# Starting the first projection from x with features on the partitions, and applying its norm factor to the products

## The chip, the cores and the metric

One core of a Trainium2 chip runs the whole program: matrix products on TensorE (PE), elementwise work on VectorE (DVE), ScalarE (ACT) and GpSimd (POOL), loads and stores issued by SyncE (SP). The metric is device time in microseconds, the median of three runs.

## What is computed

Two layers of a first block (an even one with forgetting and dilated attention, an odd one with retention), and a second block with a state-space mixer, windowed attention and a gated feed-forward part. S = 256 positions, D = 1024 features, all fp32. The change touches the start of the even layer:

```python
def rms_norm(x, g):
    y = xf * lax.rsqrt(jnp.mean(xf * xf, axis=-1, keepdims=True) + EPS)
    return (y * g).astype(x.dtype)

z = rms_norm(x, g_norm) @ w_in
qa, ka, va, ga, fa, qb, kb, vb, gb = jnp.split(z, cuts, axis=-1)
log_f = jax.nn.log_sigmoid(fa + b_f)
ya = forgetting_attention(hA(qa), hA(ka), hA(va), log_f)
```

The norm factor is one number per position, so it may be applied to a product x·g @ w after the product, row by row.

## The kernel before

Each fp32 operand is split into a high part (fp32r) and the low part that is left, and a product is made of three: high by high, high by low, low by high. For weights the class `Weights` does this tile by tile: `load` issues a 512 KB tile of [128, 1024] on SP, `_prepare` casts it on ScalarE (wh, L73) and takes the low part on VectorE (wl, L78) or, where `plan` is given a share, every second one on GpSimd. `next` keeps two tiles prepared ahead of the one in use. There are five raw buffers and six of wh and wl each, so a load waits for the low part of the tile five before it, and a cast for TensorE's last use of the tile six before it.

x is loaded by rows (positions on the partitions). `norm_transposed` squares and sums the rows (L199, L202), raises to -0.5 on GpSimd (L191), multiplies by factor and gain (L215), turns each 128x128 block on TensorE (L235) and splits the result into xTh and xTl (L242, L243). `first_xs` (L297, L304) makes the first value projection va from them, four weight tiles; `forget_gates` makes 24 small products with w_fa (L251 to L253), a chain of small steps on VectorE and ScalarE (L638 to L645), a copy of the running sums to c_f on GpSimd (L647) and a store to DRAM (L648). `fox_masks` loads these sums back, spread over the partitions (L653), and adds the causal mask on GpSimd (L656, L657); VectorE takes it up in `masked_min` (L354, L356).

Then for each group of heads `proj_ws` makes q, k and the gate g, two halves of eight pairs of products each (L263 with the high weights, L264 with the low ones), evicted by ScalarE and VectorE (L267 to L271) out of three banks, so that a half can start when the half three before it has left its bank. Scores (L346), softmax and the product with v follow one group behind.

Beside all this runs `tables_common`: angles, sines and powers for the state-space mixer far later (L394 to L405, L438 to L540), on VectorE, ScalarE and GpSimd, from the table ssm_par. Its four copies of m on GpSimd (L538) share one buffer, so each waits until SP has stored the one before (L540).

Nothing fixes the order of these on an engine except a few added order rules: a scheduler places every engine's instructions in one list, and an engine runs its list in order. SP's loads and stores are one such list too, and at most eight of them are under way.

Of the kernel before, what the change touches and what calls it, by code (L numbers as in the profile page):

```python
# [19 lines left out]
P = 128  # L20
# [16 lines left out]
KE = ("pp", "py")  # L37
XH = 2
# [7 lines left out]
class Weights:  # L46


    def __init__(self, tc, raw, par, ahead):
        self.tc, self.nc, self.raw, self.par, self.ahead = tc, tc.nc, raw, par, ahead  # L50
        self.after, self.loaded, self.loads, self.lows = [], [], 0, []
        self.jobs, self.shares, self.done, self.used = [], [], [], 0

# [5 lines left out]
    def load(self):  # L59
        ap = self.jobs[self.loads]  # L60
        self.loads += 1
        r = self.raw.tile([P, 1024], F32, tag="raw", name="wraw")
        self.nc.sync.dma_start(r[:, :ap.shape[1]], ap)
        self.loaded.append(r)

    def _prepare(self):
# [6 lines left out]
        i = nc.scalar.copy(h[:, :n], r[:, :n])  # L73
# [5 lines left out]
        self.done.append((h, lo))  # L79

# [19 lines left out]
def model_kernel(ctx: ExitStack, tc: tile.TileContext, a: dict, out: bass.AP):  # L100
# [23 lines left out]
    g_row = nrm.tile([P, D], F32, tag="gain", name="g_row")  # L124
    nc.sync.dma_start(g_row[:1, :], a["even_norm"])
    x = [res.tile([P, D], F32, name=f"x{t}") for t in range(2)]

    def load_x(t):
        for h in range(XH):
            sl = slice(h * D // XH, (h + 1) * D // XH)  # L130
            nc.sync.dma_start(x[t][:, sl], a["x"][t * P:(t + 1) * P, sl])

    load_x(0)
# [36 lines left out]

    w.load()
    load_x(1)


# [30 lines left out]
    def norm_transposed(t, g, th, tl, name, kinds=("pt", "pt"), eng=None, after=None):  # L205

        with tc.high_priority():
            xt = x[t]
            parts = [mean_square(xt[:, h * 512:(h + 1) * 512], D, name, eng if h else None) for h in range(2)]
            r = rstd_from(parts, EPS, name)  # L210
            xn = []
            for h in range(2):
                sl = slice(h * 512, (h + 1) * 512)
                xn.append(nrm.tile([P, 512], F32, tag="xn", bufs=3, name="xn"))
                V.scalar_tensor_tensor(xn[h], xt[:, sl], r, g[h], op0=ALU.mult, op1=ALU.mult)  # L215
            return transposed(xn, 8, th, tl, 0, t, kinds, after)

# [11 lines left out]
    def transposed(src, n, th, tl, k0, t, kinds=("pt", "pt"), after=None):  # L229

        m = min(4, n)
        for b, sb, kind in zip(range(0, n, 4), src, kinds):
            pt = bank(kind)
            for j in range(m):
                i = T.transpose(pt[:, j * P:(j + 1) * P], sb[:, j * P:(j + 1) * P], ident)  # L235
                if after is not None:
                    tc.add_manual_dep(i.ins, after.ins.name, NOSYNC, reason="order")
                    after = None
# [49 lines left out]
    def first_xs(mid):  # L288

        tiles = [w.next() for _ in range(4)]  # L290
        ps = [bank("pp"), bank("pp")]
        for t in range(2):
            st = slice(t * P, (t + 1) * P)
            for g in range(0, 8, 2):
                for xp in (xTh, xTl):
                    for k in range(g, g + 2):
                        m = T.matmul(ps[t], xp[:, k, st], tiles[k // 2][0][:, 512 * (k % 2):512 * (k % 2) + 512],  # L297
                                     start=xp is xTh and k == 0, stop=False)
                        if t == 0 and xp is xTh and k == 1:
                            mid(m)  # L300
        for t in range(2):
            st = slice(t * P, (t + 1) * P)
            for k in range(8):
                T.matmul(ps[t], xTh[:, k, st], tiles[k // 2][1][:, 512 * (k % 2):512 * (k % 2) + 512],  # L304
# [940 lines left out]
```

## Time and profile before

| | |
|---|---|
| three runs | 807.45, 807.53, 3086.02 us; median 807.53 |
| the profiled execution | 803.87 us, span 802.0 us |
| busy | PE 96%, DVE 74%, ACT 54%, POOL 30% of the span |
| chain that ended last | PE 84%, DVE 6%, POOL 3%, ACT 2%, DMA 2% |
| mean granted TensorE clock | 0.994 |

A share of busy time is a mean over the whole span. In the first 60 us it is different: TensorE starts late, and VectorE, busy 74% on the whole, is busy nearly all the time from 12 us on. Times below are from the span's start. In a timeline a row gives the start, the length from the first start to the last end, and in brackets how long the engine had been idle and what ended it.

### The profile page before, as it was taken

What the parts mean: (1) busy time and instruction counts of PE and PEld (TensorE: products, weight loads), DVE (VectorE), ACT (ScalarE), POOL (GpSimd) and SP (SyncE); (2) the same over time, 40 slices, a digit from 0 to 9 for tenths busy, and PEclk for the clock granted to TensorE, in tenths of its full rate; (3) what the DMA queues carried; (4) which work ended last, traced back from release to release, by engine and by line L of the source; (5) the groups of instructions that cost most, each with busy time, mean ns of one, the idle gap of its engine ahead of it and who ended that gap; (6) DMA issues with size and microseconds to landing.
All of it is one profiled execution on the core that took longest, in us unless ns stands there. A gap on an engine that the chain in (4) does not pass through costs nothing.

```text
span 802.0 us, 12045 instructions
## 1 busy us (share of the span) xinstructions
PE 773.2 (96%) x4282; PEld 637.4 (79%) x4282; DVE 596.6 (74%) x1109; ACT 431.9 (54%) x775; POOL 236.6 (30%) x274
## 2 busy tenths in 40 slices
PE   7999999999999999999999999989798999999996
PEld 5877887877887788888888887876577888888886
DVE  6987677878888458595867766698948897787433
ACT  5875665665666346354444345827545655654431
POOL 4553111006505303021202006863653333223110
PEclk9999999999999999999999999999999999999999
DMA  7676553643854557453636494853233656655431
GB/s 289 223 255 252 171 172 113 227 146 133 263 170 139 198 210 268 158 184 131 210 113 203 141 339 145 302 205 100 81 128 110 233 190 197 193 184 184 159 131 53
DMA packets 47422, 146.37 MB, mean 182 GB/s; under 512 B 5361, under 2 KB 11777, under 8 KB 47362
## 3 DMA queue, kind: packets, MB, share of 16 engines
q1 hardware_dynamic: 47362, 145.60, 53.8%
q8 instruction: 34, 0.56, 0.3%
q14 instruction: 26, 0.21, 0.1%
HBM read 137.70 MB, written 7.88 MB: 182 GB/s over the span
## 4 chain that ended last, share of the span: by engine, by line
PE 84%; DVE 6%; issue 3%; POOL 3%; ACT 2%; DMA 2%; SPq 0%; POOLq 0%; DVEq 0%; ACTq 0%
PE bpp L263 18%; PE bpp L282 12%; PE bpp L283 12%; PE bpp L286 12%; PE bpp L264 9%; PE bat L263 5%; PE bat L264 2%; PE bpy L380 2%; PE bat L346 2%; PE bpt L370 2%; DVE wl L78 1%; PE bpp L297 1%; POOL wl L78 1%; PE bpt L235 1%; DMA wraw<-in_w_va 1%
## 5 line engine op out<-in xcount | busy, mean ns | idle before, releaser
L78 DVE TENSOR_TENSOR wl<-wraw,wh 128x1024 fp32r<-128x1024 f32 x211 | 279.9, 1339 | 95.2 <-ACT wh L73 93.3
L73 ACT CAST wh<-wraw 128x1024 fp32r<-128x1024 f32 (+1 forms) x233 | 238.3, 1045 | 129.9 <-PE bpp L286 42.3
L263 PE MATMUL bpp<-xT,wh 128*128 128x512 f32 x672 | 242.2, 401 | 2.9 <-DVE q L271 2.9
L264 PE MATMUL bpp<-xT,wl 128*128 128x256 f32 x672 | 190.5, 283 | 0.0
L263 PEld LDWEIGHTS bpp<-xT,wh 128*128 128x128 f32 x672 | 126.9, 189 | 33.6 <-DVE q L271 3.6
L264 PEld LDWEIGHTS bpp<-xT,wl 128*128 128x128 f32 x672 | 127.6, 190 | 1.9 <-issue 1.2
L282 PE MATMUL bpp<-wh,xT 128*128 128x512 f32 (+1 forms) x288 | 109.3, 385 | 1.9 <-ACT xT L242 1.9
L283 PE MATMUL bpp<-wl,xT 128*128 128x512 f32 (+1 forms) x288 | 108.4, 381 | 0.0
L78 POOL TENSOR_TENSOR wl<-wraw,wh 128x1024 fp32r<-128x1024 f32 x22 | 58.0, 2638 | 90.0 <-ACT wh L73 89.9
L286 PE MATMUL bpp<-wh,xT 128*128 128x512 f32 (+1 forms) x288 | 74.2, 380 | 0.0
L282 PEld LDWEIGHTS bpp<-wh,xT 128*128 128x128 f32 x288 | 54.0, 188 | 13.8 <-ACT xT L242 2.8
L283 PEld LDWEIGHTS bpp<-wl,xT 128*128 128x128 f32 x288 | 54.2, 188 | 10.6 <-DVE wl L78 0.6
L286 PEld LDWEIGHTS bpp<-wh,xT 128*128 128x128 f32 x288 | 51.9, 188 | 10.2 <-issue 0.3
L263 PE MATMUL bat<-xT,wh 128*128 128x512 f32 x160 | 56.3, 395 | 0.0
L282 PE MATMUL bpp<-wh,yh 128*128 128x512 f32 x128 | 50.5, 400 | 0.0
L283 PE MATMUL bpp<-wl,yh 128*128 128x512 f32 x128 | 50.3, 396 | 0.0
L264 PE MATMUL bat<-xT,wl 128*128 128x256 f32 x160 | 44.4, 277 | 0.0
L286 PE MATMUL bpp<-wh,yl 128*128 128x512 f32 x128 | 35.7, 397 | 0.0
L263 PEld LDWEIGHTS bat<-xT,wh 128*128 128x128 f32 x160 | 30.0, 188 | 6.9
L1127 POOL TENSOR_TENSOR gr<-gr,Rh 128x512 f32<-128x512 f32 x10 | 19.3, 1929 | 40.3 <-ACT th L1126 40.3
L591 POOL COPY t<-kk 32x128 f32<-32x128 f32 (+1 forms) x64 | 25.9, 405 | 15.0 <-DVE kk L588 12.4
L264 PEld LDWEIGHTS bat<-xT,wl 128*128 128x128 f32 x160 | 30.1, 188 | 0.1
(390 smaller groups left out, 1268.8 us busy)
## 6 DMA issues: line engine op xcount, KB each, us to landing
wraw<-in_w_o SPq DMA_DIRECT2D x40, 512.0 KB, 4.3
wraw<-in_w_gate SPq DMA_DIRECT2D x22, 512.0 KB, 3.7
wraw<-in_w_up SPq DMA_DIRECT2D x22, 512.0 KB, 3.8
wraw<-in_w_dn SPq DMA_DIRECT2D x22, 512.0 KB, 3.7
wraw<-in_w_v SPq DMA_DIRECT2D x16, 512.0 KB, 4.5
wraw<-in_w_g SPq DMA_DIRECT2D x16, 512.0 KB, 4.2
wraw<-in_w_q SPq DMA_DIRECT2D x12, 512.0 KB, 3.3
wraw<-in_w_va SPq DMA_DIRECT2D x8, 512.0 KB, 6.1
```

The lines of the kernel that those rows point to most:

```text
L73: i = nc.scalar.copy(h[:, :n], r[:, :n])
L78: self.lows.append(eng.tensor_tensor(lo[:, :n], r[:, :n], h[:, :n].bitcast(F32), op=ALU.subtract))
L263: T.matmul(ps, h, xT2[:, k].rearrange("p a b -> p (a b)"), start=k == 0, stop=False)
L264: T.matmul(ps[:, :S], l, xTh[:, k, :], start=False, stop=k == 7)
L282: T.matmul(ps, lh[:, k0 + k, st], wh, start=first and k == 0, stop=False)
L283: T.matmul(ps, lh[:, k0 + k, st], wl, start=False, stop=False)
L286: T.matmul(ps, ll[:, k0 + k, st], wh, start=False, stop=last and k == n - 1)
L346: i = T.matmul(ps[j][:, o], q[rows, qs], k[rows, ks], start=True, stop=True)
L370: T.transpose(pt[:, j * P:(j + 1) * P], p[:, j * P:(j + 1) * P], ident)
L380: i = T.matmul(o[64 * j:64 * j + 64], v[:, b, vc], src, start=b == 0, stop=b == 1)
L591: G.tensor_copy(t0[32 * j:32 * j + 32, s, 32 * j:], kk[32 * s:32 * s + 32, :P - 32 * j])
L1127: G.tensor_tensor(two(gr), two(gr), rep2(Rh), op=ALU.mult)
```

## The change

x is also given transposed from the start (`xT`, features on the partitions, 1 MB, from the layout of the inputs), and the gain as a column per feature (`g_col`). x·g is split directly into xuh and xul, which share the buffer that later holds yh; the first four weight tiles are loaded into the buffer of yl. The first projection is made of these. Meanwhile the squares are summed over the partitions with a product by ones, and the factor is applied to that projection's products when they are evicted to v. For everything after it x is normalised in place (`normalised`), by a copy R of the factor spread over the partitions, and split into xTh and xTl.

```diff
 class Weights:
     def load(self):
...
+        if self.loads in self.given:
+            r = self.given.pop(self.loads)
+        else:
+            r = self.raw.tile([P, 1024], F32, tag="raw", name="wraw")
+        parts = 2 if self.loads == 0 else 1
...
+            m = self.nc.sync.dma_start(r[:, sl], ap[:, sl])
+            if i == 0 and parts > 1:
+                self.between()
...
+    def issue_after(self, n, i):
+        self.tc.add_manual_dep(i.ins, self.issued[n].ins.name, NOSYNC, reason="order")
...
+    warm = bank("py")
+    for n in (4, 4, 2):
+        T.matmul(warm[:, :n * P].rearrange("p (a b) -> p a b", a=n), ones, ones[:, None, :].to_broadcast([P, n, P]),
+                 start=True, stop=True)
...
+    nc.sync.dma_start(g_col, a["even_norm"])
...
     def load_x(t):
-        for h in range(XH):
...
+        w.issue_after(10, nc.sync.dma_start(x[t], a["x"][t * P:(t + 1) * P, :]))
+
+    def load_xT(k, n=2):
+        nc.sync.dma_start(xT[k // 4][:, k % 4:k % 4 + n, :], a["xT"][:, k:k + n, :])
...
-            w.plan(xs("w_v" + m, hf), SH[0] if m + str(hf) != "a0" else 2)
+            w.plan(xs("w_v" + m, hf), SH[0])
...
+    w.between = lambda: load_xT(1, 1)
+    for k in (2, 4, 6):
+        w.load()
+        load_xT(k)
+    for _ in range(5):
+        w.load()
...
+        def part(g, xp, j, first=False, last=False):
+            for k in range(g, g + 2):
+                for t in range(2):
+                    T.matmul(ps[t], xp[:, k, t * P:(t + 1) * P],
+                             tiles[k // 2][j][:, 512 * (k % 2):512 * (k % 2) + 512],
+                             start=first and k == g, stop=last and k == g + 1)
+        for g in range(0, 8, 2):
+            tiles.append(w.next())
+            part(g, xuh, 0, first=g == 0)
+            part(g, xul, 0)
+            if g:
+                part(g - 2, xuh, 1)
+        part(6, xuh, 1, last=True)
...
-        nc.sync.dma_start(sp, a["ssm_par"])
+        w.issue_after(12, nc.sync.dma_start(sp, a["ssm_par"]))
...
+    for k in range(8):
+        xk = xT[k // 4][:, k % 4, :]
+        A.activation(xuh[:, k, :], xk, AF.Copy, scale=g_col[:, k:k + 1])
+        V.scalar_tensor_tensor(xul[:, k, :], xk, g_col[:, k:k + 1], xuh[:, k, :].bitcast(F32),
+                               op0=ALU.mult, op1=ALU.subtract)
...
+        def square_sums():
+            sq = [ev.tile([P, 512], F32, tag=n, name="sq_e") for n in ("q", "k", "q", "k")]
...
+            V.tensor_tensor(sq[0], sq[0], sq[1], op=ALU.add)
+            V.tensor_tensor(sq[2], sq[2], sq[3], op=ALU.add)
+            V.tensor_tensor(sq[0], sq[0], sq[2], op=ALU.add)
+            V.tensor_tensor(sq[1][:, :S], sq[0][:, :S], sq[0][:, S:], op=ALU.add)
+            return sq[1][:, :S]
+
+        def normalised():
+            sm = square_sums()
...
+                T.matmul(pr[:, t:t + 1], sm[:, t * P:(t + 1) * P], ones[:, :1], start=True, stop=True)
+            for t in range(2):
+                rs.append(rstd_from([pr[:, t:t + 1]], EPS, "e"))
...
+                V.tensor_copy(rb, rs[t].to_broadcast([P, P]))
+                T.matmul(pr[:, t * P:(t + 1) * P], rb, ident, start=True, stop=True)
+            A.copy(R, pr[:, :S])
+            for t in range(2):
+                V.tensor_scalar(rh[t], rs[t], 0.5, None, op0=ALU.mult)
+            for k in range(8):
+                xk = xT[k // 4][:, k % 4, :]
+                V.scalar_tensor_tensor(xk, xk, g_col[:, k:k + 1], R, op0=ALU.mult, op1=ALU.mult)
+                if k % 2:
+                    xk = xT[k // 4][:, k % 4 - 1:k % 4 + 1, :]
+                    split(xTh[:, k - 1:k + 1, :], xTl[:, k - 1:k + 1, :], xk)
+            return rh
...
-                    A.mul(v[:, t, :], ps[t], 0.5)
+                    A.mul(v[:, t, :], ps[t], rh[t] if first else 0.5)
```

The lists of the engines change as follows. VectorE before, from the squares of the first half of the rows to the first low weight part (wl) and the first xTl (L243):

```order
L199 ISA junk_126,ss_e0_127<-x0_98 128x512
L199 ISA ss_e0_127 128x1
L187 SCALAR_TENSOR_TENSOR ms_e0_129<-ss_e0_124,ss_e0_127 128x1
L215 SCALAR_TENSOR_TENSOR xn_133<-x0_98,rstd_e0_131,bat_119 128x512
L215 SCALAR_TENSOR_TENSOR xn_135<-x0_98,rstd_e0_131,bat_120 128x512
L78 TENSOR_TENSOR wl_172<-wraw_102,wh_171 128x1024
L187 SCALAR_TENSOR_TENSOR ms_e1_215<-ss_e1_210,ss_e1_213 128x1
L243 TENSOR_TENSOR xT2_106<-bpt_137,xT2_106 128x4x128
```

VectorE after, from the third sum of squares (L689) to the factor: wl_231 and wl_310 are the low parts of w_qa, wl_351 and wl_357 of w_ka, wl_402 of w_ga, and ms_e is the mean square. Then, after a dozen small steps, come eight products by R (L714) and four low parts of x (L360):

```order
L689 TENSOR_TENSOR sq_e_250<-sq_e_250,sq_e_252 128x512
L92 TENSOR_TENSOR wl_231<-wraw_125,wh_230 128x1024
L92 TENSOR_TENSOR wl_310<-wraw_127,wh_309 128x1024
L690 TENSOR_TENSOR sq_e_251<-sq_e_250 128x256
L92 TENSOR_TENSOR wl_351<-wraw_129,wh_350 128x1024
L450 TENSOR_SCALAR nsinks_143<-sinks_142 128x8
L442 CAST pos_1535<-pos_i_1533 128x2
L92 TENSOR_TENSOR wl_357<-wraw_354,wh_356 128x1024
L228 TENSOR_SCALAR ms_e_265<-bpt_262 128x1
L228 TENSOR_SCALAR ms_e_270<-bpt_262 128x1
L445 TENSOR_TENSOR sm_trig_1502<-pos_1535,invf_1537 128x16
L92 TENSOR_TENSOR wl_402<-wraw_399,wh_401 128x1024
```

Before, one low weight part stood ahead of the second mean square; now nine do, four of them for tiles of the later q and k.

TensorE after, where the first projection ends (wl_199 is the low part of its last tile): the sums over the partitions (L699), the spread factor (L708), then forget gates and q, whose products read the normalised x:

```order
L320 MATMUL bpp_175<-wl_199,xu_112 128x512
L320 MATMUL bpp_176<-wl_199,xu_112 128x512
L699 MATMUL bpt_262<-ones_94,sq_e_251 128x1 x2
L708 MATMUL bpt_276<-ident_87,rb_e_277 128x128
L708 MATMUL bpt_276<-ident_87,rb_e_280 128x128
L274 MATMUL bpp_308<-xT2_131,wh_214 16x256
L275 MATMUL bpp_308<-xT2_131,wh_214 16x256
L276 MATMUL bpp_308<-xT2_131,wl_215 16x256
```

Before, the forget gates' products stood among and right behind those of the first projection; now all 24 stand behind the factor.

GpSimd after, from the second of the four copies m4 to c_f (c2_f): rc and rs wait for a sine, rv for powers made on VectorE:

```order
L563 COPY m4_1628<-sm_mag4_1621 128x256
L564 MEMSET m4_1628 128x4
L496 COPY rc_140<-sm_trig_1502 128x16
L497 COPY rs_141<-sm_trig_1502 128x16
L563 COPY m4_1632<-sm_mag4_1621 128x256
L564 MEMSET m4_1632 128x4
L524 COPY rv_r_1582<-pw_r_1562 128x16
L525 COPY rv_i_1583<-pw_i_1563 128x16
L563 COPY m4_1636<-sm_mag4_1621 128x256
L564 MEMSET m4_1636 128x4
L524 COPY rv_r_1582<-pw_r_1562 128x16
L667 COPY c2_f_346<-c_f_344 16x2x32x4
```

The list before has the same order from the first copy to c_f. What differs is when the copies' input comes: ssm_par is loaded behind the second pair of w_qa tiles now, where before it was issued ahead of the first, and mag4 is made behind L360.

## Rows read from the trace of the kernel before

**Rows 1.** The page's chain that ended last: shares of the span by engine.

```profile
PE 84%; DVE 6%; issue 3%; POOL 3%; ACT 2%; DMA 2%; SPq 0%; POOLq 0%; DVEq 0%; ACTq 0%
```

**Rows 2.** Timeline of TensorE: start, us, engine, line, operation, out<-in, count, idle before.

```profile
10.83 2.07 PE L297 MATMUL bpp<-wh,xT 128*128 128x512 f32 x4 [1.78 <-ACT xT L242]
...
24.80 0.28 PE L251 MATMUL bpp<-xT,wh 128*16 128x256 f32 x1
...
27.21 0.40 PE L263 MATMUL bpp<-xT,wh 128*128 128x512 f32 x1
...
45.05 0.93 PE L346 MATMUL bat<-k,q 64*128 64x128 f32 x8
...
60.92 0.50 PE L263 MATMUL bpp<-xT,wh 128*128 128x512 f32 x1 [2.41 <-DVE q L271]
...
62.68 0.63 PE L263 MATMUL bpp<-xT,wh 128*128 128x512 f32 x1
...
63.32 0.63 PE L263 MATMUL bpp<-xT,wh 128*128 128x512 f32 x1
```

**Rows 3.** Stretches: us, busy us of each engine, granted clock, DMA share, GB/s.

```profile
30.00:35.00 5.00, 5.00 (x31) 4.35 (x30) 5.00 (x13) 3.41 (x5) 3.80 (x4) 1.00 0.93 311
58.50:60.90 2.40, 0.01 (x1) 0.00 (x0) 2.40 (x7) 1.29 (x2) 0.75 (x2) 1.00 1.07 399
62.00:65.30 3.30, 3.30 (x13) 2.82 (x12) 3.30 (x12) 0.63 (x3) 2.08 (x3) 0.52 0.88 326
```

**Rows 4.** Timeline of VectorE.

```profile
28.32 1.21 DVE L78 TENSOR_TENSOR wl<-wraw,wh 128x1024 fp32r<-128x1024 f32 x1
...
39.07 0.67 DVE L397 SCALAR_TENSOR_TENSOR trig<-trig 128x512 f32<-128x512 f32 x1
...
53.85 0.29 DVE L354 CUSTOM_DVE_ANT_0 s<-bat,m 128x128 f32<-128x128 f32 x1 [2.41 <-POOL m L656]
...
60.46 0.41 DVE L271 SCALAR_TENSOR_TENSOR q<-bpp,q 128x256 f32<-128x256 f32 x1
```

**Rows 5.** Timeline of GpSimd (spans on this engine are rough).

```profile
10.58 0.56 POOL L191 TENSOR_TENSOR rstd_e<-ms_e,mhalf 128x1 f32<-128x1 f32 x1 [4.34 <-DVE ms_e L187]
...
20.21 0.40 POOL L538 COPY m<-sm_mag 128x256 f32<-128x256 f32 x1 [2.21 <-DVE sm_mag L534]
...
24.51 0.50 POOL L538 COPY m<-sm_mag 128x256 f32<-128x256 f32 x1 [3.73 <-DMA w_dram<-m]
...
31.36 2.82 POOL L499 COPY rv_r<-pw_r 128x16 f32<-128x16 f32 x1
...
35.02 5.34 POOL L538 COPY m<-sm_mag 128x256 f32<-128x256 f32 x1 [0.71 <-DMA w_dram<-m]
...
44.83 0.65 POOL L647 COPY c_f<-c_f 16x256 f32<-16x256 f32 x1 [3.73 <-DVE c_f L645]
```

**Rows 6.** Timeline of SyncE's issues.

```profile
2.47 0.91 SPq L131 DMA_DIRECT2D x<-in_x  x2
3.42 1.82 SPq L63 DMA_DIRECT2D wraw<-in_w_va  x3
...
26.92 0.43 SPq L540 DMA_DIRECT2D w_dram<-m  x1
...
45.50 0.32 SPq L648 DMA_DIRECT2D c_dram<-c_f  x1
```

**Rows 7.** The tile x, 0 to 14 us: its four loads.

```profile
DMA to landing us min/median/max: 2.6/4.6/6.4
```

**Rows 8.** The tensor in_w_va, 0 to 14 us: its four loads.

```profile
DMA to landing us min/median/max: 6.0/7.2/8.0
```

**Rows 9.** Timeline of ScalarE.

```profile
19.39 2.93 ACT L73 CAST wh<-wraw 128x1024 fp32r<-128x1024 f32 x3
...
23.18 0.60 ACT L665 ACTIVATE v<-bpp 128x512 f32<-128x512 f32 x1 [0.86 <-PE bpp L304]
...
30.24 0.38 ACT L270 ACTIVATE q<-bpp 128x256 f32<-128x256 f32 x1 [1.56 <-PE bpp L264]
```

More of the change, by code (lines that the diff above doesn't have):

```diff
@@ L52, in __init__ @@
         self.jobs, self.shares, self.done, self.used = [], [], [], 0
+        self.issued, self.given, self.casts = [], {}, []
     def plan(self, aps, share=0):
@@ L72, in _prepare @@
         lo = self.par.tile([P, 1024], F32R, tag="wl", name="wl")
-        i = nc.scalar.copy(h[:, :n], r[:, :n])
+        if not self.done:
+            nc.scalar.copy(h[:, :n // 2], r[:, :n // 2])
+            i = nc.scalar.copy(h[:, n // 2:n], r[:, n // 2:n])
+        else:
+            i = nc.scalar.copy(h[:, :n], r[:, :n])
+        self.casts.append(i)
         if self.after:
@@ L203, in mean_square @@
         return s
[L205 to L216, printed above, removed]
     def gained_transposed(t, g, kinds):
@@ L234, in transposed @@
             for j in range(m):
[L235 to L238, printed above, removed]
+                T.transpose(pt[:, j * P:(j + 1) * P], sb[:, j * P:(j + 1) * P], ident)
             pv = pt[:, :m * P].rearrange("p (j t) -> p j t", j=m)
@@ L286, in mm_xs, with first_xs @@
                 T.matmul(ps, ll[:, k0 + k, st], wh, start=False, stop=last and k == n - 1)
-    def first_xs(mid):
-        tiles = [w.next() for _ in range(4)]
+    def first_xs():
         ps = [bank("pp"), bank("pp")]
[L292 to L304, printed above, removed]
-                         start=False, stop=k == 7)
+        tiles = []
+        def part(g, xp, j, first=False, last=False):
[11 more added lines that the diff above has]
+        part(6, xuh, 1, last=True)
         return ps
@@ L601, in tables_quarter @@
         nc.sync.dma_start(y_dram[i][:, QT0:], t0.rearrange("p s c -> p (s c)"))
-    g_even = [bank("at") for h in range(2)]
-    for h in range(2):
-        T.matmul(g_even[h], ones[:1, :], g_row[:1, h * 512:(h + 1) * 512], start=True, stop=True)
-    norm_transposed(0, g_even, xTh, xTl, "e0", eng=V)
-    def second_tile(after):
-        norm_transposed(1, g_even, xTh, xTl, "e1", KE, None, after)
-    lctx = ExitStack()
-    ypool = lctx.enter_context(tc.tile_pool(name="ypool", bufs=1))
+    for k in range(8):
[3 more added lines that the diff above has]
+                               op0=ALU.mult, op1=ALU.subtract)
     def y_tiles():
@@ L660, in model_kernel @@
         for mi, m in enumerate(("a", "b")):
             for hf in range(2):
-                ps = proj_xs(xTh, xTl, 8) if mi or hf else first_xs(second_tile)
+                first = not (mi or hf)
+                ps = first_xs() if first else proj_xs(xTh, xTl, 8)
+                if first:
+                    rh = normalised()
+                    yh, yl = y_tiles()
                 v = ev.tile([P, 2, 512], F32, tag="v", name="v")
                 for t in range(2):
-                    A.mul(v[:, t, :], ps[t], 0.5)
@@ L666, in model_kernel @@
-                if mi == 0 and hf == 0:
+                    A.mul(v[:, t, :], ps[t], rh[t] if first else 0.5)
+                if first:
                     forget_gates()
                 for i in range(2):
-                    qk = []
                     q = ev.tile([P, 2, S], F32, tag="q", name="q")
@@ L673, in model_kernel @@
                     proj_ws(k)
+                    if first and not i:
+                        w.issue_after(6, nc.sync.dma_start(masks, a["c_masks"]))
+                        for t in range(2):
+                            load_x(t)
                     gp = ev.tile([P, 2, S], F32, tag="gp", bufs=1, name="gp")
```

45 lines of the change are left out of this document (30 added, 15 removed).

## Prediction

> **What bounds the kernel now.** I read the chain of waits first: TensorE is 84% of it [rows 1], so a microsecond reaches the end only by way of TensorE's order. The change touches only the first 61 us of that order, so I read TensorE's timeline there. Its first real product starts at 10.83, the forget gates' last 21 of 24 small products run from 24.80 to 27.21, and the first q projection starts at 27.21 [rows 2]. By then the first projection and the forget gates are both done. The scores start at 45.05. From there TensorE runs on to one real stop: at 60.92 it has waited 2.41 us for an eviction by VectorE (a q, L271) [rows 2]. The table of stretches says why and what follows: VectorE is busy all of 30 to 35 and all of 58.5 to 60.9, and TensorE, idle for those 2.4 us, has a granted clock of 0.52 (its lower level) from 62.0 to 65.3 [rows 3]. A pair of products L263, L264 then takes 0.64 us (62.68 to 63.32). At full clock it takes 0.355 (27.21 to 45.05 holds 48 pairs, a wait of 0.52 and 0.3 of other gaps) [rows 2]. So the stop costs 2.4 and then about 1.45 (five pairs).
>
> VectorE, saturated, had itself stood for 2.41 us before 53.85, until GpSimd handed over the first forget mask [rows 4]. GpSimd's timeline shows where that comes from: the copy of the gates' sums, c_f, starts at 44.83 [rows 5], its store is issued at 45.50 [rows 6], and the mask returns by a load: 9.0 us from c_f's copy to VectorE's first use at 53.85.
>
> **What the change does to the start.** *Loads.* Before, 3.0 MB (x and four weight tiles) must land, the last of them issued at about 4.4 and landed 8.0 later, at 12.4 [rows 6, 7, 8]. After, 3.07 MB must land in smaller pieces, first among them 128 KB of x and half a weight tile. By the same landings, in order of bytes: 1.54 MB at 9.3 (x's last piece before: issued 2.9, plus 6.4 [rows 6, 7]), the last tile at 12.5. So the last weight does not come sooner; what can come sooner is the work ahead of it.
>
> *ScalarE.* From the second weight tile at 9.3 it has no gap: three casts of 0.98 (three in 2.93 [rows 9]), three squares of 0.53 and four products of 0.3 (0.60 and 0.38 as shown, less 0.08 of overlap [rows 9]). The fourth tile's cast ends at 15.6. TensorE follows with 16 products and has the first projection done by about 19.5, where before it was near 25. So far the change does what it says.
>
> *VectorE.* Lengths below are those shown less the 0.08 that overlaps the next row: 1.13 for a weight's low part, 0.60 for 128x512, 0.33 for 128x256 [rows 4]. From the third tile's cast (13.45) it runs, in the order printed in the section on the change: low part 14.6, two x products 15.25, sum 15.85, fourth low part (cast 15.6) 17.0, w_fa's 17.3, sum 17.9, **two low parts of w_qa 20.15**, sum 20.5, **w_ka** 21.6, two small ones 21.8, **w_ka** 22.95, then the two mean squares 23.15. The scheduler has put four weight tiles ahead of the norm factor: 4.5 us. GpSimd's two powers take 0.56 each [rows 5] and end at 24.3, under a fifth low part (w_ga, 24.3). Four small ones: 24.9. ScalarE first scales the two products (v, 0.55 each), then copies R: 26.2. Eight products of 0.33 give 28.9, the first xTl 0.6 more: **29.5**. The second matrix product of the forget gates needs it, so TensorE stands from 19.5 to 29.5.
>
> That is not all loss, as five weight tiles are ready by then. But of the work that stood before 27.21, the forget gates (24 of 0.113: 2.7 us) are still to do, and after ten idle microseconds I charge the lower clock once more, 1.45, by the stop at 58.5. Then 48 pairs, 16.9: scores at 50.6 against 45.05, **5.5 later**.
>
> *Given back.* Before, TensorE came to the seventh q/k/g half after the scores at 58.5 and got past it at 60.92, then lost 1.45: as good as 62.4. After, four halves (11.3), two groups of scores (0.86 each) and no wait: 63.7. So with VectorE in time the net is **+1.3**.
>
> *Is VectorE in time?* It needs the mask. The gates' scan ends 48.4 by the same sums: VectorE leaves the x work at 31.3, has 4.5 us of angle work, z at 36.1, then evictions, low parts and angle steps as before. 48.4 + 9.0 gives 57.4, and the eviction that TensorE needs comes 6.0 later (7.0 before, 53.85 to 60.87 [rows 4], less 1.0 for a product of w2 that now stands behind it): 63.4, in time. But c_f's copy stands on GpSimd behind four copies of m4, which need ssm_par's table and so start after the x work, at 33.0 in place of 20.21. Before, they were over at 40.4, 20.2 later (35.02 + 5.34) [rows 5], and nothing waited behind them. After, c_f does. Each copy waits for the store of the one before, 3.9 us with its issue (20.61 to 24.51). Their own lengths are 0.40 on a quiet VectorE and up to 5.34 on a full one; a column copy took 2.82, c_f 0.65 [rows 5]. Bounds for c_f's start: 48.4 (copies of 0.4 each; not late) and 54.5 (three of 3 to 5 us). I take the run before as the nearest: 20.2, less 1.5 for the second store, issued at 26.92 [rows 6] for a copy done at 25.0 because a weight's wait stood ahead of it on SP, as none does now, and one column copy, taken as long as c_f's own 0.65: 33.0 + 18.7 + 0.6 = **52.3**. Mask at 61.3, eviction at 67.3, TensorE past it at 67.3 against 62.4: **+4.9 us**.
>
> What a blocked copy costs is where the Trainium skill differs from the row. The row: a 128x256 copy lasted 5.34 us beside a full VectorE [rows 5], whose longest instruction is 1.21 [rows 4]. The skill's page "SBUF — State Buffer" (Who interferes with whom) says that GpSimd and a VectorE instruction with two SBUF inputs hold a shared port for one whole instruction and the other waits until it ends. By that rule a copy would lose about one VectorE instruction, 1.2 us, c_f would start near 50 and the change cost about 3 (its chance is inside that of the in-time case below); by the row it loses several, which my 4.9 rests on.
>
> *At no cost:* x as rows (1 MB) is loaded later and needed only at the first layer's end. On SP's queue it now stands, with seven weight tiles, ahead of ssm_par: 9.0 MB in all, 5.9 of them after 12.5, at 311 to 399 GB/s [rows 3], so ssm_par lands at 27.3 to 31.5. VectorE asks for it at 31.3: covered, barely. The warming products depend on nothing and end before 5.5. GpSimd no longer makes two low parts; VectorE makes them, 2.3, counted above. Behind about 90 us every engine has the same order, but for one stretch near 560 us where the attention and gating steps change places; the same work stands ahead of the gate there, so nothing, give or take 1.
>
> **The rivals.**
> *In time* (+1.3): GpSimd's copies stay near 0.5, as the first two were, 0.40 and 0.50 [rows 5]. The mask waits for the scan alone. 805.2 profiled, 808.8 as median.
> *Faster* (-2.8): if loads are never late, VectorE's own list up to the first xTl is 20.1 us of work from 4.0 (nine low parts 10.2 and w_fa's 0.3, sixteen x products 5.3, sums 2.1, small ones 1.6, the first xTl 0.6), plus 1.4 for R: 25.5, not 29.5. All else moves with it: 63.7 less 4 is 59.7 against 62.4. Against it: the landings [rows 7, 8]. 804.7 as median. It also bounds the gain, as no row lets VectorE do that list in less.
> *Slower* (+8.4): GpSimd stays shut out, each copy as long as the 5.34. Decisive from c_f's start at 54 on: mask 63.3, eviction 69.3, and TensorE after its long stop at the lower clock again, 1.45. For it: VectorE is full without a gap from 31 to 57. 815.9.
> *That the normalising is not "meanwhile"* is no rival but my forecast: it stands behind the projection, not beside it.
>
> **The numbers.** The sum is made against the profiled execution, 803.9 us (span 802.0). The median shown is 807.5, 3.6 above it. Adding the same difference: 807.5 + 4.9 = **812.4**. Chances: forecast (+3 to +7) 0.45, in time 0.25, slower 0.16, faster 0.12, anything larger 0.02. The unknown landings move TensorE's return by 1.2 either way. Leaving out half of the faster and of the slower case gives 805.3 to 816.5. Two per cent, 16 us, is about what a measurement of this kernel tells from no change: no case reaches it. So within 2%: 0.96; slower 0.03 (a second wait that I don't see); faster 0.01, since even the first 27 us can't shrink by 16.
>
> **What would show it.** First product near 5; first projection done by 20; TensorE idle until 29 to 30, released by VectorE's L360; lower clock after it; scores near 50.6. Then c_f's copy at 52, VectorE idle before L379 for about 4 us released by GpSimd's L676, TensorE stopped near 60 and again at 66. If c_f starts by 49, the in-time case holds. If L714 starts before 24, the sum over VectorE's list is wrong.

## The result, and the profile after

The kernel with the change takes 820.0 us (median of four runs, 819.3 to 821.7) against 807.7: ratio 1.0154, interval 1.0127 to 1.0182, **12.4 us slower**. The forecast was 812.4, the range 805.3 to 816.5. The sign was right, and so was "within 2%"; the forecast size was two fifths of the measured one.

The profiled run of the change took 819.5 us (span 817.7), 0.5 below its median; that of before lay 3.6 below its own. So of the 15.5 us between the two traces about 3 are the draw. Read against the trace of before at the same work, the change is 8.4 us late at 108 us, 9.2 at 248, 10.1 at 534, 13.7 at 639 and 15.5 at 734. It loses in three places: at the start, from about 540 to 640 us, where the order of some instructions also changed, and in the feed-forward stage behind that, by a slow creep.

**The start.** TensorE's timeline of the change (start, us, engine, line, operation, out<-in, count, idle before), against [rows 2]:

```profile
5.27 0.73 PE L320 MATMUL bpp<-wh,xu 128*128 128x512 f32 x2 [0.25 <-ACT wh L83]
...
19.10 2.03 PE L320 MATMUL bpp<-wl,xu 128*128 128x512 f32 x8
21.53 0.60 PE L699 MATMUL bpt<-ones,sq_e 128*128 128x1 f32 x4 [0.40 <-DVE sq_e L690]
25.98 1.31 PE L708 MATMUL bpt<-ident,rb_e 128*128 128x128 f32 x4 [3.84 <-DVE rh L711]
29.32 0.39 PE L274 MATMUL bpp<-xT,wh 128*16 128x256 f32 x1 [2.03 <-ACT xT L359]
31.64 0.39 PE L275 MATMUL bpp<-xT,wh 128*16 128x256 f32 x1 [1.93 <-DVE xT L360]
...
52.80 0.93 PE L371 MATMUL bat<-k,q 64*128 64x128 f32 x8
65.35 0.55 PE L286 MATMUL bpp<-xT,wh 128*128 128x512 f32 x1 [2.95 <-DVE q L294]
```

The first product starts at 5.27 where 10.83 stood; the first projection ends at 21.1. Then TensorE stands until 31.64 but for nine small products. The scores come at 52.80, 7.75 later than the 45.05 of [rows 2], and a stop of 2.95 us at 62.4 to 65.35 answers to the 2.41 before 60.92 (it stands one half of q, k or g earlier in TensorE's order). The 7.75 and the 0.54 by which the new stop is longer than the old one add up to 8.3, which is the shift near 100 us. The table of stretches of the change (us, busy us of each engine, granted clock, DMA share, GB/s) shows the lower clock (0.5 is 1.2 GHz of 2.4) after both, as [rows 3] showed it after the one stop of before:

```profile
25.00:30.00 5.00, 1.71 (x5) 1.10 (x5) 4.20 (x19) 2.80 (x5) 1.18 (x2) 0.50 1.02 413
30.00:35.00 5.00, 3.36 (x13) 2.72 (x14) 4.93 (x22) 1.73 (x5) 0.42 (x2) 0.51 0.51 204
62.40:65.30 2.90, 0.00 (x0) 0.00 (x0) 1.72 (x8) 2.87 (x4) 2.48 (x4) 1.00 0.91 220
65.30:68.60 3.30, 3.25 (x11) 2.81 (x12) 3.30 (x8) 3.27 (x10) 3.05 (x4) 0.55 1.01 377
```

Where the ten idle microseconds come from stands in VectorE's timeline of the change, against [rows 4]: low parts of weights (L92) ahead of the mean squares (L228) and one more behind them, the x products (L714) only from 27.73.

```profile
18.79 2.35 DVE L92 TENSOR_TENSOR wl<-wraw,wh 128x1024 fp32r<-128x1024 f32 x2
...
23.80 0.22 DVE L228 TENSOR_SCALAR ms_e<-bpt 128x1 f32<-128x1 f32 x2
...
24.02 1.22 DVE L92 TENSOR_TENSOR wl<-wraw,wh 128x1024 fp32r<-128x1024 f32 x1
...
27.73 3.25 DVE L714 SCALAR_TENSOR_TENSOR xT<-xT,g_col,Re 128x256 f32<-128x256 f32 x8
...
49.83 0.67 DVE L665 TENSOR_TENSOR_SCAN c_f<-ones,z_f 16x256 f32<-16x256 f32 x1
...
63.58 0.29 DVE L379 CUSTOM_DVE_ANT_0 s<-bat,m 128x128 f32<-128x128 f32 x1 [4.26 <-POOL m L676]
```

And GpSimd's timeline of the change, against [rows 5]:

```profile
24.11 2.07 POOL L230 TENSOR_TENSOR rstd_e<-ms_e,mhalf 128x1 f32<-128x1 f32 x2 [21.16 <-DVE sm_trig L445]
...
42.00 4.22 POOL L497 COPY rs<-sm_trig 128x16 f32<-128x16 f32 x1
...
47.66 4.02 POOL L525 COPY rv_i<-pw_i 128x16 f32<-128x16 f32 x1
...
51.63 0.98 POOL L563 COPY m<-sm_mag 128x256 f32<-128x256 f32 x1
...
53.24 2.76 POOL L667 COPY c_f<-c_f 16x256 f32<-16x256 f32 x1
62.82 0.72 POOL L676 TENSOR_TENSOR m<-m,masks 128x256 f32<-128x256 f32 x1 [6.82 <-DMA m<-c_dram]
```

The two powers took 2.07, where one alone took 0.56. The gates' scan was over at 50.5; its copy c_f started 2.7 later, behind the column copies (rs, rv) and the copies m4, and lasted 2.76 instead of 0.65. The mask then kept VectorE waiting 4.26 us.

**The creep.** Between 660 and 690 us, in the feed-forward stage, both kernels run the same pairs of products (one with the high weights, wh, one with the low ones, wl) without a gap at granted clock 1.00. First and last product with wh in that stretch, of before (87 such rows) and of the change (86):

```profile
659.91 0.40 PE L263 MATMUL bpp<-xT,wh 128*128 128x512 f32 x1
...
689.73 0.40 PE L263 MATMUL bpp<-xT,wh 128*128 128x512 f32 x1
```

```profile
659.86 0.40 PE L286 MATMUL bpp<-xT,wh 128*128 128x512 f32 x1
...
689.89 0.40 PE L286 MATMUL bat<-xT,wh 128*128 128x512 f32 x1
```

One pair takes 29.82 / 86 = 0.347 us before and 30.03 / 85 = **0.353** after: 2% slower, in work that the change does not touch. One step of the feed-forward (32 pairs) goes from 11.09 to 11.31 us. The kernel has 832 such pairs, so 832 x 0.0065 = 5.4 us is a bound for them, not their price: early in before many pairs take 0.353 already. Its first eight, from 27.21 [rows 2] on, do; the eighth starts at 29.68, 7 x 0.353 later.

```profile
29.68 0.40 PE L263 MATMUL bpp<-xT,wh 128*128 128x512 f32 x1
```

### The profile page after: what moved, and what is told of

Its sections match the earlier page's. It is cut to its first block, busy times and chain, and to the rows that moved or that the text cites. A ratio compares the mean times of both kernels' runs of the same rounds, so it can differ in the third digit from the quotient of the medians.

```text
span 817.7 us, 12072 instructions
## 1 busy us (share of the span) xinstructions
PE 783.2 (96%) x4276; PEld 643.0 (79%) x4276; DVE 604.3 (74%) x1129; ACT 439.4 (54%) x786; POOL 231.7 (28%) x272
## 5 line engine op out<-in xcount | busy, mean ns | idle before, releaser
L92 DVE TENSOR_TENSOR wl<-wraw,wh 128x1024 fp32r<-128x1024 f32 (+1 forms) x209 | 276.4, 1335 | 98.4 <-ACT wh L86 96.9
L86 ACT CAST wh<-wraw 128x1024 fp32r<-128x1024 f32 (+1 forms) x229 | 234.0, 1044 | 133.2 <-PE bpp L309 43.6
L286 PE MATMUL bpp<-xT,wh 128*128 128x512 f32 x672 | 245.0, 404 | 3.0 <-DVE q L294 3.0
L305 PE MATMUL bpp<-wh,xT 128*128 128x512 f32 (+1 forms) x288 | 110.5, 390 | 1.1 <-ACT xT L265 1.0
L92 POOL TENSOR_TENSOR wl<-wraw,wh 128x1024 fp32r<-128x1024 f32 x20 | 51.4, 2574 | 90.4 <-ACT wh L86 90.3
L309 PE MATMUL bpp<-wh,xT 128*128 128x512 f32 (+1 forms) x288 | 74.9, 382 | 0.0
L305 PE MATMUL bpp<-wh,yh 128*128 128x512 f32 x128 | 50.5, 399 | 0.0
L388 ACT ACTIVATE s<-s,nm 128x128 f32<-128x128 f32 x40 | 15.9, 397 | 25.9 <-DVE nm L379 17.5
```

The source lines that it names most:

```text
L92: self.lows.append(eng.tensor_tensor(lo[:, :n], r[:, :n], h[:, :n].bitcast(F32), op=ALU.subtract))
L286: T.matmul(ps, h, xT2[:, k].rearrange("p a b -> p (a b)"), start=k == 0, stop=False)
L305: T.matmul(ps, lh[:, k0 + k, st], wh, start=first and k == 0, stop=False)
L309: T.matmul(ps, ll[:, k0 + k, st], wh, start=False, stop=last and k == n - 1)
L388: A.activation(p[:, :P], s[:, :P], AF.Exp, bias=nm[:, 0:1], scale=-1.0, accum_out=dn[:, 0:1])
```

## The experiments

All ratios are to the kernel before, timed on the same chip. Differences in us are those of the ratios, times 807; the change itself is at 1.0154.

**1. Is the slower pair real?** Before again, unchanged.

> The kernel before, unchanged, to have a second profile of it. The trace of the change runs 8.4 us behind the trace of before at 108 us, 10.1 behind at 541, 13.7 at 639 and 15.5 at 734, and only 12.3 of that is in the medians. Theory: some 3 us of the growth belong to the one profiled execution of before (803.9 against a median of 807.7), so this profile will be near 807 and its gating steps of the last stage (L1126) will come every 11.3 us, as in the change, and not every 11.1. Rival: before is steady and the growth is all the change's; then the profile reads 804 again. Time against before: 0.

805.8 us, ratio 0.9995 [0.9981, 1.001], its step 11.095. The slower pair belongs to the change. Its profile ran 1.9 behind the first one of before from 639 us on, so the first was a quick draw by that much. It took 805.75, the median of its runs, so it is the better trace to compare with: against it the change is 7.5 late at 100 us, 8.3 at 430, 11.8 at 641 and 13.6 at 735.

**2. The gates' copy, c_f, moved from GpSimd to VectorE**, with eight of VectorE's instructions ordered behind it, and one store of m behind its store.

```
-            G.tensor_copy(c2.rearrange("p (t j c) -> p t c j", t=2, j=4), natural(c))
+            V.tensor_copy(c2.rearrange("p (t j c) -> p t c j", t=2, j=4), natural(c))
```

> The change, with the copy of the gates' sums (c_f) made by VectorE right behind the scan instead of by GpSimd, and its store issued ahead of the fourth m4 store on SP. Nothing else moves before 50 us, and nothing behind 100 us. Theory (the mask is late because c_f's copy stands behind the table copies on GpSimd): c_f is ready at 51 in place of 56.0, the mask comes near 58, VectorE's wait of 4.26 for it and TensorE's wait of 2.95 at 62.4 are gone, and so is the lower clock after it; 3 to 5 us faster than the change, 815 to 817. Rival (the 10 us in which TensorE stands for the norm factor are the loss, the mask only fills slack that this leaves): under 1 us faster, and TensorE stops at the same place for something else.

817.0 us, 1.0130 [1.0111, 1.0149]: 1.9 better than the change. The intervals overlap, but the trace agrees: 5.7 behind before again at 100 us, where the change was 7.5 behind. VectorE's and GpSimd's timelines of it:

```profile
52.01 0.41 DVE L667 COPY c_f<-c_f 16x256 f32<-16x256 f32 x1
...
60.36 0.29 DVE L379 CUSTOM_DVE_ANT_0 s<-bat,m 128x128 f32<-128x128 f32 x1
```

```profile
43.23 4.28 POOL L563 COPY m<-sm_mag 128x256 f32<-128x256 f32 x1
...
59.58 0.74 POOL L676 TENSOR_TENSOR m<-m,masks 128x256 f32<-128x256 f32 x1 [7.61 <-DMA m<-c_dram]
```

and what TensorE waited for in it at 60 to 75 us:

```profile
PE bpp L286 <- DVE q L294: 0.5, 1, 0.5
```

L379 now has no wait before it; TensorE's stop shrinks from 2.95 to 0.5, and its granted clock is 1.00 from 60 to 70. So the late copy caused the stop. It was worth half of what the theory said. In this one execution the scores came 1.3 later than the change's (54.09), although no order differs before 50 us: the granted clock was still 0.76 from 35 to 40 us, where the change had 1.00.

**3. The late order.** The scheduler had also changed the order of instructions near 560 us. Here the stretch is held in before's order (LATE lists its 147 instructions), and in a second kernel before gets the change's order there.

```
+    for row in LATE:
+        for m, n in zip(row, row[1:]):
+            tc.add_manual_dep(by[f"I-{n}"], f"I-{m}", NOSYNC, reason="order")
```

> The change, with the order of the late stretch (attention heads and gating of the last block, about 120 instructions of TensorE, VectorE and ScalarE near 550 to 590 us) forced to that of the kernel before; everything else as in the change. The trace of the change falls 2 us further behind between 541 and 584 us. Theory (the reordering costs that): 2 to 3.5 us faster than the change. Rival (the reordering costs nothing, what grows there is TensorE's granted clock after stops, which falls differently from run to run): within 1 us of the change.

> The kernel before, with the late stretch forced into the order that it has in the change, the start untouched. Theory (the reordering costs 2 to 3.5): 809.7 to 811.2 where before is 807.7. Rival (it costs nothing, as the prediction said): within 1 us of before.

818.0 us, 1.0141 [1.0124, 1.0159], and 807.2 us, 1.0018 [1.0004, 1.0033]: 1.0 better and 1.4 worse. The first interval overlaps that of the change and the second only just leaves out no difference, but they agree in sign and size: the order costs about 1. The traces say less evenly how much. From 432 to 641 us the change falls 3.5 us back against before again and the first of these kernels 2.9; the second, with before's places, falls 1.7 back. The second kernel's step stays 11.095, so the order has nothing to do with the slower pair.

**4. Where the weight buffers lie.** The change allocates a column of norm weights and a small tile ahead of the weights' raw, high and low buffers, so each of these lies 64 bytes higher; the first high one begins at byte 38304 of each partition, not 38240. Before, with 64 unused bytes there:

```
+    pad = const.tile([P, 16], F32, name="pad")
+    G.memset(pad[:, :1], 0.0)
```

> The kernel before with one more constant tile of 64 bytes per partition (written once, read never) ahead of the weight buffers; every engine's order is that of before, but for one memset on GpSimd. It puts the weight buffers 64 bytes higher, where the column g_col puts them in the change. At one and the same granted clock of 1.00 a pair of products L263, L264 comes every 0.347 us in the feed-forward stage of three profiles with the old places (before, before again, before with the late order of the change), and every 0.353 in three with the new ones (L286, L287 in the change and its two variants); a step of the stage takes 11.10 and 11.31. Theory (where the buffers lie sets that pace): 0.353 and 11.31 here too, and 4 to 6 us slower than before (672 + 160 pairs by 0.0065 are 5.4). Rival (something else in the changed program sets it, such as its loads or its timing): 0.347, 11.10, and within 1 us of before.

810.7 us, 1.0052 [1.0029, 1.0075]: **4.2 us for 64 unused bytes**. The same stretch of its timeline (86 products):

```profile
659.89 0.40 PE L265 MATMUL bat<-xT,wh 128*128 128x512 f32 x1
...
689.92 0.40 PE L265 MATMUL bpp<-xT,wh 128*128 128x512 f32 x1
```

30.03 / 85 = 0.353, as in the change. TensorE's order in this trace is that of before again, product by product, so the two can be compared over the whole span. The 747 distances from pair to pair that nothing interrupts (under 0.4 us) add up to 260.87 us there and 263.63 here: 2.8, half of the 5.4. Some products that hold the weights still and move x are slower too. These are rows of before again and of this run, from the table of groups (busy us, mean ns of one):

```profile
L283 PE MATMUL bpp<-wh,xT 128*128 128x512 f32 x256 | 101.1, 397 | 3.3 <-ACT xT L243 3.3
L284 PE MATMUL bpp<-wh,xT 128*128 128x512 f32 x256 | 102.6, 403 | 1.6 <-ACT xT L244 1.6
```

Against before again it falls 3.1 back from 432 to 641 us and 1.8 from there to 735.

The reverse, the change with its two tiles allocated behind the buffers:

```
-    warm = const.tile([P, 1], F32, name="warm")
+    warm = nrm.tile([P, 1], F32, tag="warm", bufs=1, name="warm")
...
-    g_col = const.tile([P, 8], F32, name="g_col")
+    g_col = nrm.tile([P, 8], F32, tag="g_col", bufs=1, name="g_col")
```

> The change, with its two new small constants (the gain column g_col, 32 bytes per partition, and the 4-byte tile of the warming copy) allocated behind the weight buffers instead of ahead of them. The weight buffers then lie where they lie in before; every engine's order is exactly that of the change. Theory (their 64 bytes cost 4 us by the pace of the products): pairs at 0.347, steps of the feed-forward stage at 11.10, 4 us faster than the change, a ratio to before of 1.009 to 1.012. Rival (it was another buffer behind the weights that the 64 bytes moved; those stay moved here): as the change, pairs at 0.353, 1.0154.

814.3 us, 1.0107 [1.0083, 1.0131]: 3.8 better. Its 87 products in that stretch:

```profile
659.86 0.39 PE L286 MATMUL bpp<-xT,wh 128*128 128x512 f32 x1
...
689.67 0.39 PE L286 MATMUL bpp<-xT,wh 128*128 128x512 f32 x1
```

29.81 / 86 = 0.347. Both directions agree: the place of the buffers is 4 us of the 12.4. Compared with the change, only the weights' raw, high and low buffers (and four small tables) lie elsewhere in this kernel. So it is the weights' buffers that count, but no run separates the three kinds. Nor is their place all that counts: with the first high buffer at 38240 in both, this kernel ran the second to fifth half of the first q, k and g at 0.347, and before ran them at 0.353.

Which places are good? Three more: the change with 64 bytes more (the pad above), and before with 32 and with 160.

> The change with the same 64 bytes more, so that its weight buffers lie 128 bytes above those of before. Orders as in the change, but for one memset. Theory (the places set the pace, and what counts repeats every 128 bytes): pairs at 0.347, steps of 11.10, 4 to 6 us faster than the change, a ratio to before of 1.008 to 1.011. If what counts does not repeat at 128, pairs stay at 0.353 or come at a third value. Rival (places don't matter): as the change, 1.0154.

> The kernel before with 32 unused bytes per partition ahead of the weight buffers; orders as in before, but for one memset. The high weights' first buffer then starts at byte 38272 of the partition, a multiple of 128; in before it is 38240, with 64 unused bytes 38304 (both 32 past a multiple of 64), in the change with 64 more 38368. Theory A (what counts is the start against a multiple of 64 or 128, and an even start is the best): pairs of products below 0.347 and 2 us or more faster than before. Theory B (what counts is something that moves with every 32 bytes, such as which other buffers are read and written at the same low address bits): a value between 0.347 and 0.353, time from the same to 4 us slower.

> The same with 160 unused bytes: the first buffer at 38400, a multiple of 512. Theory A: as with 32 bytes or better, 2 us or more faster than before. Theory B: any value from 0.347 to 0.353 with no relation to that with 32 bytes. If the pace depended on the distance moved alone, it would be the slowest of all.

1.0158 [1.0132, 1.0183], 1.0031 [1.0012, 1.0050] and 1.0040 [1.0020, 1.0060]; steps 11.24, 11.10 and 11.20. No multiple sorts the places into good and bad. With 32 bytes most halves at 112 to 180 us ran at 0.353 and the feed-forward at 0.347, and before itself has halves of both kinds there; with 64 all run at 0.353. And the step does not give the time: with 32 bytes it is that of before, yet the kernel is 2.5 us slower. That the place changes the pace is shown; why is open.

**5. The norm factor earlier.** The prediction charged 4.5 us of weights' low parts ahead of the factor. Two kernels put some of them behind it (both with the change's late order held). First, four low parts of w_qa and w_ka behind the mean squares:

```
+        if self.pin and len(self.done) < 9:
+            self.tc.add_manual_dep(self.lows[-1].ins, self.pin, NOSYNC, reason="order")
...
+            w.pin = ms.ins.name
+            tc.add_manual_dep(w.lows[5].ins, w.pin, NOSYNC, reason="order")
```

> The change with the four low parts of w_qa and w_ka on VectorE put behind the two mean squares of the norm factor; the late stretch is held in the order of the change. Theory (TensorE's long stop is the norm factor's wait, and the work behind it moves with it): mean squares at 21.7 in place of 23.8, TensorE back with the second product of the forget gates at 29.5 in place of 31.6, and the table copies on GpSimd and the mask, which follow the x work, 1.5 to 2 earlier as well: 1 to 2 us faster than the change. Rival (the mask's chain holds the end and does not move): TensorE is back at 29.5 and stops longer near 62, time within 0.5 us of the change.

823.4 us, 1.0205 [1.0181, 1.0228]: 4 worse. (Its profiled execution took 819.7, 3.4 less than any other of its six, so its trace shows less than these 4.) GpSimd's, VectorE's and TensorE's timelines of it:

```profile
23.05 2.59 POOL L245 TENSOR_TENSOR rstd_e<-ms_e,mhalf 128x1 f32<-128x1 f32 x2 [20.10 <-DVE ms_e L243]
```

```profile
22.88 3.48 DVE L105 TENSOR_TENSOR wl<-wraw,wh 128x1024 fp32r<-128x1024 f32 x3
...
27.56 0.22 DVE L725 COPY rb_e<-rstd_e 128x128 f32<-128x128 f32 x1
```

```profile
33.49 0.39 PE L290 MATMUL bpp<-xT,wh 128*16 128x256 f32 x1 [2.01 <-DVE xT L375]
```

The low parts then ran beside the powers, which took 2.59, and ahead of the factor's copy: TensorE came back at 33.49. The work had been moved into the wait, not out of it. So the second kernel puts two behind the last sum of squares and three behind the factor's last copy (L720):

```
+    for n, m in ((233, 261), (312, 261), (353, 285), (359, 285), (404, 285)):
+        tc.add_manual_dep(by[f"I-{n}"], f"I-{m}", NOSYNC, reason="order")
```

> The change with VectorE's start in another order: the two low parts of w_qa behind the last sum of squares (which then is ready at 19.5), and the two of w_ka and one of w_ga behind the factor's last copy, so that none stands between the mean squares and the factor; the late stretch held in the order of the change. Theory: mean squares near 22, factor at 24.8 in place of 26.5, TensorE back at 30 in place of 31.6, table copies and mask 1.5 earlier too: 1 to 2 us faster than the change, 1.0130 to 1.0145. Rival (VectorE is the bound there, what is put behind comes back as later products): TensorE back at 31 or later, no gain.

818.3 us, 1.0152 [1.0131, 1.0172]: no gain, as the rival said. Its GpSimd, VectorE and TensorE:

```profile
22.74 1.07 POOL L243 TENSOR_TENSOR rstd_e<-ms_e,mhalf 128x1 f32<-128x1 f32 x2 [19.79 <-DVE nsinks L463]
```

```profile
24.05 2.35 DVE L105 TENSOR_TENSOR wl<-wraw,wh 128x1024 fp32r<-128x1024 f32 x2
...
26.40 1.22 DVE L105 TENSOR_TENSOR wl<-wraw,wh 128x1024 fp32r<-128x1024 f32 x1
27.53 3.25 DVE L727 SCALAR_TENSOR_TENSOR xT<-xT,g_col,Re 128x256 f32<-128x256 f32 x8
```

```profile
31.53 0.40 PE L288 MATMUL bpp<-xT,wh 128*16 128x256 f32 x1 [2.02 <-DVE xT L373]
```

The powers took 1.07, the factor was there at 24.1, and the x products still began at 27.53, behind the same low parts. In this kernel the factor is not the bound; VectorE's list is.

The powers agree with the Trainium skill, "SBUF — State Buffer" (Who interferes with whom), by which GpSimd and a VectorE instruction with two SBUF inputs shut each other out for one whole instruction: the two took 2.59 beside low parts of 1.2, and 1.07 beside short ones. The copies do not: 4.22 and 4.02 in the change and 4.28 in experiment 2 are each longer than three of VectorE's longest instructions. There the measurement decides.

**6. No factor at all.** The norm factor replaced by a constant.

```
-            A.copy(R, pr[:, :S])
+            A.copy(R.rearrange("p (a b) -> p a b", a=2), ones[:, None, :].to_broadcast([P, 2, P]))
...
-                V.tensor_scalar(rh[t], rs[t], 0.5, None, op0=ALU.mult)
+                V.tensor_scalar(rh[t], ones[:, :1], 0.5, None, op0=ALU.mult)
```

> The change with the norm factor replaced by a constant 1 where x and the first products take it: squares, sums and powers still run, but nothing waits for them, so the values are those without the norm. It prices the wait for the factor. Theory (TensorE's stop from 21 to 31.6 at the lower clock is the larger part of the loss before 108 us): TensorE is back near 26, the scores stand near 46.5 in place of 52.8, and the time is 4 to 6 us below the change, 1.008 to 1.0105. Rival (VectorE's list and the mask bound the stretch to 70 us in any case): scores earlier, but a longer stop near 62; under 2 us faster, 1.013 or more.

816.7 us, 1.0126 [1.0107, 1.0146]: 2.3 better, between the two and nearer the rival (the intervals overlap; at 100 us its trace is 1.9 ahead of the change's). TensorE came back at 28.71, 2.9 earlier. This is not the price of the wait alone: with nothing to wait for, the scheduler also put the x products ahead of four of the low parts (they start at 20.92) and c_f's copy ahead of two copies m4 (it starts at 42.94), so the stop near 62 shrank as well. Without the factor, and with the order that this allows, 2.3 us come back.

**7. All at once**: tiles moved (4), the start's order (5, second), c_f on VectorE (2), late order of before (3).

> All four together: the constants behind the weight buffers, the order of the start as in the last experiment, c_f copied by VectorE behind the scan, and the late stretch in the order of before. Theory (the parts are separate and add up): 4 for the places, 1.5 for the order of the start, 2 for the copy, 1 for the late order: 8.5 of the 12.3, a ratio to before of 1.004 to 1.007. Rival (they overlap, as TensorE waits for the next of them at the same place): 1.009 or more.

811.9 us, 1.0056 [1.0035, 1.0077]: 7.9 of the 12.4 come back. The 8.5 of the expectation counted 1.5 for the start's order, which gave 0.2 by itself; measured one by one the parts gave 3.8, 0.2, 1.9 and 1.0, that is 6.9. Of its TensorE timeline, and its wait at 60 to 75 us:

```profile
30.19 0.40 PE L288 MATMUL bpp<-xT,wh 128*16 128x256 f32 x1 [2.02 <-DVE xT L373]
```

```profile
PE bpp L299 <- DVE q L307: 0.8, 1, 0.8
```

One wait of 0.8 is left there, and the clock is 1.00 from 60 to 70. From 432 to 641 us this kernel keeps its distance to before again. The change fell 3.5 back there, the 64 bytes alone 3.1, and the late order with the buffers put back (the reverse in experiment 4) 3.5. So by these traces, one of each, places and late order hide each other in that stretch, and taking away one of them gives back little of it. It is the best form of the change, and still slower than before.

**8. The same with x first**: the low parts of w_ka and w_ga also behind those of x, by two numbers in the list above (285 to 301).

> The four edits together as before, and on VectorE the two low parts of w_ka and the one of w_ga behind the four low parts of x instead of ahead of the products by the factor. Theory (with the factor at hand near 23, VectorE's list is what holds TensorE): products by the factor start near 25 in place of 26.2, TensorE is back at 28.7 in place of 30.2, and the time is 1 to 2 us below that of the four edits, a ratio to before of 1.003 to 1.0045. Rival (ScalarE's two products v and the copy of the factor come next, or the later low parts are then missed by q and k): TensorE back at 29.5 or later, or back early and stopped again before 50; within 0.7 us of the four edits.

817.9 us, 1.0139 [1.0110, 1.0168]: 6.7 worse than experiment 7. TensorE, SyncE, VectorE and TensorE's waits at 60 to 75 us:

```profile
27.63 0.39 PE L288 MATMUL bpp<-xT,wh 128*16 128x256 f32 x1 [1.93 <-DVE xT L373]
```

```profile
21.24 9.67 SPq L82 DMA_DIRECT2D wraw<-in_w_qa  x2
30.96 0.91 SPq L469 DMA_DIRECT2D ssm_par<-in_ssm_par  x1
```

```profile
37.40 0.18 DVE L477 TENSOR_SCALAR ssm_par<-ssm_par 128x16 f32<-128x16 f32 x1 [4.61 <-DMA ssm_par<-in_ssm_par]
```

```profile
PE bpp L299 <- DVE q L307: 3.9, 1, 3.9
```

TensorE was back 2.6 us earlier than in experiment 7 and lost it all. Low parts made later hold their raw buffers longer; SyncE's two loads of w_qa, which need such a buffer, took 9.67 us to issue; ssm_par, queued behind, was issued at 30.96; VectorE waited 4.61 for it; what VectorE owed came late, and TensorE stopped 3.9 us at 65 to 70, with a granted clock of 0.50 from 70 to 75. (In experiment 7 the same load was issued at 24.33.)

## Why the prediction was wrong

**The step that failed** is "Behind about 90 us every engine has the same order ... so nothing, give or take 1". The order was what it said, and its one changed stretch costs about 1 by the times of experiment 3; the traces leave room for more. But "nothing" took for granted that a product whose instruction is unchanged costs what it cost. Two new tiles ahead of the weight buffers moved them by 64 bytes. The pairs of the feed-forward took 2% longer, other products less, and the program 4 us more (experiment 4). The prediction had no rival for it and no room in its range.

The start costs the rest. By subtraction, 12.4 less 4 and 1, it is about 7.4 where 4.9 stood. The traces bear this out only roughly: against before again the change is 7.5 late at 100 us, and the change with its buffers put back 5.8. Step by step:
- *First product near 5, first projection by 20, ScalarE and TensorE in time:* right but for a microsecond (5.27 and 21.1). ScalarE's terms as listed add up to 15.0, not to the 15.6 that the text goes on with; the fourth cast ended at 16.5. The forecast that the norm stands behind the projection and not beside it: right.
- *TensorE back at 29.5:* 31.64. Mis-sized terms: the mean squares were done at 24.0 for 23.15, and the powers took 2.07 for the 1.12 taken from a quiet row [rows 5], though the same paragraph had a low part beside them. The eight x products took 3.2 for 2.7. Lower clock after it: right. Scores 52.80 for 50.6.
- *Four halves and two groups of scores up to the stop:* right, but the half at which TensorE stopped before is the fifth behind the scores, not the seventh.
- *c_f behind GpSimd's copies:* mechanism right, confirmed by experiment 2. Its start, 53.24 for 52.3, and the mask's arrival at VectorE, 63.58 for 61.3: c_f itself was blocked and lasted 2.76, where 0.65 was taken, with the row of 5.34 beside a full VectorE in hand. VectorE idle "about 4": 4.26, right.
- *TensorE stopped near 60 and again at 66:* one stop, to 65.35. And the sum charged no lower clock behind it, although [rows 3] shows 0.52 behind a stop of 2.41: 0.55 it was, so the 1.45 of that row belonged in the sum. How the forecast shift of 4.9 became 8.4 at 108 us can't be split exactly, as the stop came at another half of the work; by the rows it is the scores' 7.75 and the 0.54 of the longer stop. About 0.8 of the 8.4 is the quick draw of before.
- *ssm_par covered, barely:* right; it was no wait in the change, and one of 4.61 in experiment 8, as soon as SyncE's queue slipped.

Of the rivals, "in time" and "faster" did not occur. "Slower" (+8.4) comes nearest: its condition, c_f as late as 54, was in effect met when the copy ended at 56.0, and its lower clock came. It had 0.16. That its 8.4 is also the shift at 108 us is in part luck, as it had the scores at 50.6. "Faster" named 25.5 as VectorE's own bound; experiment 8 got to 27.63 and paid for it elsewhere.

What stays after all repairs is 4.5 us (experiment 7). Its one profiled execution, 3.7 quicker than its median, is 3.0 behind before again at 100 us and 2.1 at 641, so as far as a trace shows it lies in the start. Experiments 5, 6 and 8 narrow down what it is: doing without the factor gave 2.3, and moving the parts of VectorE's list ahead of the second product only moved the wait. That the list itself is the rest, the two low parts that GpSimd made before among it, is argued from this and not shown; no run made it shorter.

## What to carry to other kernels

A new tile allocated ahead of large buffers moves them: compare the pace of an unchanged instruction far from the edit before explaining a difference by order or waits, and allocate small additions behind the buffers, so that these stay where they were. Charge a long stop of TensorE with the clock that follows it, also where the stop is only moved: here 0.52 and 0.55 behind stops of 2.41 and 2.95 us, and 1.00 throughout around those of 0.5 and 0.8. On an engine that is full, putting one thing first decides what waits next; ask which buffer that instruction would have freed, and what is queued behind its load.

## What the runs showed that was not expected

The pace of products with the same operands in shape and type depends on where the weights' buffers lie. In the feed-forward a pair takes 0.347 us with the first high buffer at byte 38240 in six profiles, 0.353 at 38304 in seven, 0.351 at 38368, 0.350 at 38400 and 0.347 at 38272. Earlier in the program it is 0.353 throughout at 38304, and 0.347 or 0.353, by the stretch, at 38240 and 38272. The page "SBUF — State Buffer" of the Trainium skill (Who interferes with whom) has only the port pair of VectorE and GpSimd as a cause of contention; whether contention is the cause here no run shows. And two powers on 128x1 columns took 1.07 to 2.59 us by what VectorE did beside them.
